# Attention stage without elementwise work on GpSimd, and low weight parts by an adding DMA

## The chip, the cores and the metric

The kernel runs on one core of a Trainium2 chip. The metric is the device time of one execution in microseconds, the median of several runs. The engines are TensorE (PE, with its weight loads shown as PEld), VectorE (DVE), ScalarE (ACT), GpSimd (POOL) and SyncE (SP), which here only issues DMAs.

## The reference

One block of a bidirectional encoder on 512 tokens of width 1024, with 16 learned meta tokens in front, in float32:

```python
u = rms_norm(h, pre_mix_gain)
qa, ka, va, qb, kb, vb, g = split(u @ w_in)         # rope on qa, ka, qb, kb
o_swa  = windowed_gqa_sink_attention(qa, ka, va, sink)   # 16 heads of 64, 4 kv heads, +-128 and meta keys
o_diff = differential_attention(qb, kb, vb, lam)    # 8 heads: (softmax(q1 k1) - lam softmax(q2 k2)) v,
                                                    # then RMS norm of each head
gates = sigmoid(g + b_gate)
merged = gates[:D] * (o_swa @ w_branch_swa) + gates[D:] * (o_diff @ w_branch_diff)
h = h + rms_norm(merged @ w_out)
f = (silu(gate) * up) @ w_ffn_out                   # gate, up = rms_norm(h) @ w_ffn_in, 2816 wide each
h = h + rms_norm(f)
```

## The kernel before, in words

Every float32 operand of a large product is split into a high part that TensorE multiplies at full speed (`float32r`) and a low part, the difference. A product is hi\*hi + hi\*lo + lo\*hi, summed in PSUM (`mm3`, L139-144). Activations lie with features on the partitions (`xh`, `xl`: 8 slices of 128 features by 528 tokens); a projection is 8 slices of 3 matmuls into one PSUM bank `pr` (`proj_g`, L146).

**Weights** come in tiles of 128 x 1024 floats (512 KB) by `load_w` (L124): SP loads `raw` (tile `wr`, 3 buffers), ACT casts it to the high part `wh` (L130), and the low part `wl` = raw - wh is a subtraction in `sub_hi` (L110). For the 4th to the 51st call POOL does three quarters of that subtraction (768 columns) and DVE the last quarter (256); for all others DVE does all 1024. `wh` and `wl` have 3 buffers each, so ACT can write the parts of a load when the product three loads back has ended.

**Windowed attention** (`s_swa`, L448, and `t_swa`, L502) runs over 16 units, each a query block of 128 tokens by 4 heads. Per head TensorE makes scores (L465), DVE adds the mask and takes the minimum (L468; scores are negated), and ACT takes the exponential with its sum (L471). The sink sits in one more column of the tile `p`, which POOL fills head by head (L467). Then DVE inverts the sums and POOL scales the four heads' probabilities (L476). TensorE transposes them (L516), ACT casts the high part `ah` (L115), DVE makes the low part `al` (L111), and TensorE multiplies them by V (L530-534).

**Differential attention** (`s_diff`, L607, and `t_diff`, L645) runs over 8 heads of 4 query blocks with two score maps each: scores `Sd` into one double bank (L626), minimum `dnm` on DVE (L629), exponential on ACT (L630). For a query block DVE makes the two factors `drc` (L634-635), POOL scales the first map (L636) and DVE adds the second (L638, tile `pa` or `pp`). After transposes and the products with V the head is normed over its rows: square on ACT, its low part `sl` on POOL (L683), a power by logarithm and exponential, and a Newton step with three operations on POOL (L699-701) and one on DVE (L702).

**Rotary embedding** (`rope`, L321): two products on DVE (`ta`, `tb`, L325-326), their sum on POOL (L327), then a split into `hl` on ACT and DVE (L118-119), from which SP's DMAs build the operands `Q`, `Qd`, `Kd`. It is called 26 times.

**Fillers.** Between the steps of attention TensorE takes projections: queries, keys and values of coming heads (`f_q`, `f_qk`, `f_vd`), the gates (`f_gate`, 8 beside windowed attention and 8 near the end of the differential branch in `f_gate2`), and the product with `w_branch_swa` (`f_b1`, 8 tiles, beside the first heads). The class `Order` (L35) fixes in which order TensorE takes all these pieces, from written costs and delays; that order does not depend on the other engines' code. On DVE, ACT, POOL and SP a scheduler orders the instructions after the first part of the kernel when the program is built, each queue then running in that order.

After about 550 us the branch products, the output projection and the FFN follow, with no such interleaving.

Of the kernel before, what the change touches and what calls it, by code (L numbers as in the profile page):

```python
# [12 lines left out]
F32 = mybir.dt.float32  # L13
# [7 lines left out]
P = 128  # L21
# [74 lines left out]
def encoder(ctx, tc, I, out, dbg=None):  # L96
# [25 lines left out]
    nw = [0]  # L122

    def load_w(src, k=KT, dst=None):  # L124
        raw = wp.tile([P, k, D // k], F32, tag="wr", name="wr", bufs=RB)
        sp.dma_start(out=raw, in_=src.rearrange("p (k c) -> p k c", k=k))
        if dst is None:
            dst = [wp.tile([P, k, D // k], F32R, tag=t, name=t) for t in ("wh", "wl")]
        wh, wl = dst
        act.copy(out=wh, in_=raw)  # L130
        # during attention the vector engine is the busiest: GpSimd takes three quarters of the low parts
        nw[0] += 1
        cut = 3 * k // 4 if 4 <= nw[0] < 52 else 0
        if cut:
            sub_hi(wl[:, 0:cut], raw[:, 0:cut], wh[:, 0:cut], pool)
        sub_hi(wl[:, cut:], raw[:, cut:], wh[:, cut:])
        return wh, wl
# [18 lines left out]
    def rsqrt_cols(pl, ss, n, scale, tag, extra=None, bufs=1):  # L156
        """(ss*scale + eps)^-0.5 on [n, m] columns, with one Newton step; extra replaces eps."""
        m = ss.shape[1]
        v, h, y, z = (pl.tile([P, m], F32, tag=tag + c, name=tag + c, bufs=bufs) for c in "vhyz")
        if extra is None:  # L160
            dve.tensor_scalar(out=v[:n], in0=ss, scalar1=scale, scalar2=EPS, op0=ALU.mult, op1=ALU.add)
        else:
            dve.scalar_tensor_tensor(out=v[:n], in0=ss, scalar=scale, in1=extra, op0=ALU.mult, op1=ALU.add)  # L163
        pool.tensor_tensor(out=y[:n], in0=v[:n], in1=mhalf[:n, 0:m], op=ALU.pow)  # L164
        dve.tensor_scalar(out=h[:n], in0=v[:n], scalar1=-0.5, scalar2=1.0, op0=ALU.mult, op1=ALU.mult)
        if m == 1:
            dve.scalar_tensor_tensor(out=z[:n], in0=y[:n], scalar=h[:n], in1=y[:n], op0=ALU.mult, op1=ALU.mult)
        else:
            dve.tensor_tensor(out=z[:n], in0=y[:n], in1=y[:n], op=ALU.mult)
            dve.tensor_tensor(out=z[:n], in0=z[:n], in1=h[:n], op=ALU.mult)  # L170
        dve.scalar_tensor_tensor(out=y[:n], in0=z[:n], scalar=1.5, in1=y[:n], op0=ALU.add, op1=ALU.mult)
        return y

# [14 lines left out]
    zero = const.tile([P, 256], F32, name="zero")  # L188
# [4 lines left out]
    RB = 3  # L193
# [18 lines left out]
    # the tensor engine's clock rises only under load  # L212
# [59 lines left out]
    # K of the windowed branch, slice by slice as x arrives; then V  # L272
# [13 lines left out]
    # row statistics of x: 1/rms, broadcast to all partitions  # L286
# [28 lines left out]
    # small vectors  # L315
# [5 lines left out]
    def rope(hl, psa, psb, c0, n, o0, scale=None):  # L321
        """psa, psb: [P, n] products of columns c0..c0+n; hl[:, part, hi/lo, o0..o0+n] gets the rotated split."""
# [4 lines left out]
        pool.tensor_tensor(out=ta, in0=ta, in1=tb, op=ALU.add)  # L327
# [53 lines left out]
    def v_swa(VT):  # L381
# [6 lines left out]
        act.copy(out=m, in_=zero[0:48, :].rearrange("p (a b c) -> p a b c", a=2, b=2))  # L388
# [43 lines left out]
    # per query block: (key column range, mask, [(offset in range, key block or -1 for meta)])  # L432
# [10 lines left out]
    # meta rows of the transposed probabilities; the gaps between the row groups stay zero  # L443
    aTm = atp.tile([80, 512], F32R, tag="am", name="aTm")
    for c in range(2):
        act.copy(out=aTm[:, c * 256:(c + 1) * 256], in_=zero[0:80, :])

    def s_swa():  # L448
        for u in range(16):
# [9 lines left out]
            pt = atp.tile([P, 4, 401], F32, tag="p", name="p", bufs=2)  # L459
            for hh in range(4):  # L460
# [6 lines left out]
                pool.tensor_copy(out=p[:, nk:nk + 1], in_=nsink[:, h:h + 1])  # L467
# [7 lines left out]
            for hh in range(4):  # L475
                pool.tensor_scalar(out=pt[:, hh, 0:nk], in0=pt[:, hh, 0:nk], scalar1=rc[:, hh:hh + 1],  # L476
                                   scalar2=1.0, op0=ALU.mult, op1=ALU.mult)
# [5 lines left out]
    def pipe(n, tr_fn, av_fn, done_tr, free_at):  # L483
        """tr_fn(k), then av_fn(k, operand): two transposed banks ahead."""
# [64 lines left out]
    def f_gate(j, dst):  # L549
        w = load_w(I["w_in"][36 + j])  # L550
# [33 lines left out]
    def f_vd(h):  # L584
# [8 lines left out]
        def finish():  # L593
# [5 lines left out]
            act.copy(out=m, in_=zero[0:80, 0:P])  # L599
# [7 lines left out]
    def s_diff():  # L607
        for h in range(8):
# [8 lines left out]
            for i in range(4):  # L617
# [4 lines left out]
                for c in range(2):  # L622
                    S = ps.tile([P, 2, 512], F32, tag="S", name="Sd")
                    for s in range(2):
                        for x in range(2):
# [10 lines left out]
                pool.tensor_scalar(out=pc[0], in0=pc[0], scalar1=rc[:, 0:1], scalar2=1.0,  # L636
                                   op0=ALU.mult, op1=ALU.mult)
# [7 lines left out]
    def t_diff():  # L645
        free_at = 0.0
        for h in range(8):
# [28 lines left out]
            # per-head RMS norm over the 128 rows of O  # L676
# [6 lines left out]
            split(sh, sl, sq, eng=pool)  # L683
# [15 lines left out]
            pool.tensor_tensor(out=z, in0=y, in1=y, op=ALU.mult)  # L699
            pool.tensor_tensor(out=z, in0=z, in1=v, op=ALU.mult)  # L700
            pool.tensor_scalar(out=z, in0=z, scalar1=-0.5, scalar2=1.5, op0=ALU.mult, op1=ALU.add)
            dve.tensor_tensor(out=y, in0=y, in1=z, op=ALU.mult)  # L702
# [21 lines left out]
    def f_b1(j):  # L724
        w = load_w(I["w_bs"][j])
# [68 lines left out]
    # the eight banks as two sets of four  # L794
# [25 lines left out]
    # all of w_out stays on chip, in the space of the hidden activations  # L820
# [236 lines left out]
```

## Time and profile before

| | |
|---|---|
| three runs | 1016.4, 1016.48, 1017.12 us (median 1016.48) |
| span of the profiled execution | 1015.2 us |
| busy TensorE | 973.6 us (96%) |
| busy DVE, ACT, POOL | 589.3, 446.8, 246.8 us |

The time listed is that of the runs; for the profiled execution only its span is given. "Busy" counts instructions at work; matmuls are pipelined and their ends modelled, so TensorE's busy time hides short waits. A row of a group shows line, engine, operation, tiles (out<-in), shapes and count, then busy time and mean ns, then idle time before and what ended it. A row of the timeline shows start and duration in us, and in brackets the engine's idle time before it with what it waited for.

### The profile page before, as it was taken

The numbers are of one execution on the slowest core, as the hardware profiler recorded it, in microseconds if no ns is written. First come the engines' busy times: TensorE is split into PE (matmuls) and PEld (weight loads), VectorE is DVE, ScalarE is ACT, GpSimd is POOL, SyncE is SP. The second block draws the span as 40 slices with busy tenths as digits, with TensorE's granted clock in tenths as the row PEclk, the third lists the DMA queues.
The fourth block names the chain that finished last, engine by engine and source line by source line (L and its number), as shares of the span: only waits on it lengthen the run. The fifth ranks groups of instructions, "written<-read, shape, count | busy, mean of one in ns | idle before, by whom it ended". The sixth has DMA issues, their size and how long they took to land.

```text
span 1015.2 us, 14301 instructions
## 1 busy us (share of the span) xinstructions
PE 973.6 (96%) x5355; PEld 830.5 (82%) x5355; DVE 589.3 (58%) x979; ACT 446.8 (44%) x820; POOL 246.8 (24%) x294
## 2 busy tenths in 40 slices
PE   9989999989999997998999999999999999999997
PEld 9767777869888887988887888998888888888885
DVE  5856788766675868788874574863333333322224
ACT  6336677565443654654556352543233233222121
POOL 1443454534434554543421000100000000000000
PEclk9998999999999999998999999999999999999999
DMA  9572131341515144233512471353323323324122
GB/s 329 157 196 71 43 83 43 92 117 46 146 61 147 43 126 123 57 100 100 145 59 90 134 230 56 112 175 104 102 86 104 102 84 104 102 86 145 57 68 83
DMA packets 36597, 109.33 MB, mean 108 GB/s; under 512 B 5921, under 2 KB 6433, under 8 KB 35889
## 3 DMA queue, kind: packets, MB, share of 16 engines
q1 hardware_dynamic: 36528, 108.42, 35.3%
q8 instruction: 42, 0.69, 0.3%
q14 instruction: 27, 0.21, 0.1%
HBM read 87.04 MB, written 2.10 MB: 88 GB/s over the span
## 4 chain that ended last, share of the span: by engine, by line
PE 73%; DVE 12%; DMA 4%; issue 4%; ACT 4%; POOL 2%; SPq 1%; DVEq 0%; ACTq 0%; POOLq 0%
PE pr L142 15%; PE pr L143 15%; PE pr L144 15%; PE wk L142 2%; PE wk L143 2%; PE wk L144 2%; PE tr L516 2%; DMA wr<-in_w_in_dram 2%; PE Sd L626 2%; DVE wl L111 2%; PE Sw L465 2%; PE acc L143 1%; PE tr L143 1%; PE acc L142 1%; PE tr L142 1%
## 5 line engine op out<-in xcount | busy, mean ns | idle before, releaser
L130 ACT CAST wh<-wr 128x1024 fp32r<-128x1024 f32 x134 | 140.7, 1051 | 279.1 <-PE pr L143 122.2
L111 DVE TENSOR_TENSOR wl<-wr,wh 128x1024 fp32r<-128x1024 f32 (+2 forms) x138 | 153.1, 1110 | 138.3 <-ACT wh L130 130.5
L142 PE MATMUL pr<-xh,wh 128*128 128x264 f32 (+1 forms) x616 | 199.9, 325 | 0.0
L143 PE MATMUL pr<-xl,wh 128*128 128x264 f32 (+1 forms) x616 | 197.7, 321 | 0.7 <-DVE xl L234 0.7
L144 PE MATMUL pr<-xh,wl 128*128 128x264 f32 (+1 forms) x616 | 197.4, 320 | 0.7 <-DVE wl L111 0.7
L144 PEld LDWEIGHTS pr<-xh,wl 128*128 128x128 f32 x616 | 117.0, 190 | 9.3 <-DVE wl L111 0.9
L143 PEld LDWEIGHTS pr<-xl,wh 128*128 128x128 f32 x616 | 117.2, 190 | 7.1 <-DVE xl L234 1.2
L142 PEld LDWEIGHTS pr<-xh,wh 128*128 128x128 f32 x616 | 117.1, 190 | 6.9 <-issue 1.2
L111 POOL TENSOR_TENSOR wl<-wr,wh 128x768 fp32r<-128x768 f32 x48 | 95.6, 1992 | 86.9 <-ACT wh L130 85.0
L142 PE MATMUL pr<-uh,wh 128*128 128x512 f32 (+1 forms) x304 | 110.8, 364 | 0.0
L143 PE MATMUL pr<-ul,wh 128*128 128x512 f32 (+1 forms) x304 | 110.6, 364 | 0.0
L144 PE MATMUL pr<-uh,wl 128*128 128x512 f32 (+1 forms) x304 | 110.6, 364 | 0.0
L164 POOL TENSOR_TENSOR r3y<-r3v,mhalf 128x1 f32<-128x1 f32 x4 | 2.2, 552 | 352.7 <-DVE r3v L163 352.7
L142 PEld LDWEIGHTS pr<-uh,wh 128*128 128x128 f32 x304 | 57.3, 189 | 9.1
L144 PEld LDWEIGHTS pr<-uh,wl 128*128 128x128 f32 x304 | 57.4, 189 | 9.1
L143 PEld LDWEIGHTS pr<-ul,wh 128*128 128x128 f32 x304 | 57.4, 189 | 9.0
L629 DVE TENSOR_REDUCE dnm<-Sd 128x1 f32<-128x528 f32 x64 | 44.9, 702 | 22.8 <-PE Sd L626 22.5
L626 PE MATMUL Sd<-Kd,Qd 128*128 128x264 f32 x256 | 44.4, 295 | 9.6 <-ACT pp L630 8.0
L471 ACT ACTIVATE p<-p,nm 128x273 f32<-128x273 f32 (+1 forms) x64 | 36.9, 576 | 30.9 <-DVE nm L468 21.9
L468 DVE CUSTOM_DVE_ANT_0 p<-Sw,mk,nsink 128x272 f32<-128x272 f32 (+1 forms) x64 | 36.0, 563 | 24.3 <-PE Sw L465 22.9
L327 POOL TENSOR_TENSOR ta<-ta,tb 128x528 f32<-128x528 f32 (+1 forms) x26 | 35.7, 1372 | 55.0 <-DVE tb L326 46.4
L626 PEld LDWEIGHTS Sd<-Kd,Qd 128*128 128x128 f32 x256 | 36.7, 191 | 14.4 <-ACT pp L630 11.4
(370 smaller groups left out, 1979.3 us busy)
## 6 DMA issues: line engine op xcount, KB each, us to landing
wr<-in_w_in_dram SPq DMA_DIRECT2D x50, 512.0 KB, 3.8
wr<-in_w_fi_dram SPq DMA_DIRECT2D x50, 512.0 KB, 3.5
wr<-in_w_fo_dram SPq DMA_DIRECT2D x22, 512.0 KB, 3.5
Kd<-hl SPq DMA_DIRECT2D x32, 132.0 KB, 2.4
Kd<-Kd SPq DMA_DIRECT2D x8, 528.0 KB, 4.3
Q<-hl SPq DMA_DIRECT2D x64, 64.0 KB, 2.0
Qd<-hl SPq DMA_DIRECT2D x64, 64.0 KB, 2.1
wr<-in_w_bs_dram SPq DMA_DIRECT2D x8, 512.0 KB, 3.5
```

The costliest lines, as they stand in the source:

```text
L111: (eng or dve).tensor_tensor(out=lo, in0=src, in1=hi.bitcast(F32), op=ALU.subtract)
L130: act.copy(out=wh, in_=raw)
L142: pe.matmul(out=ps, lhsT=ah, rhs=bh, start=first, stop=False)
L143: pe.matmul(out=ps, lhsT=ah, rhs=bl, start=False, stop=False)
L144: pe.matmul(out=ps, lhsT=al, rhs=bh, start=False, stop=last)
L327: pool.tensor_tensor(out=ta, in0=ta, in1=tb, op=ALU.add)
L465: pe.matmul(out=S, lhsT=Qs[g][hh // 2][:, hh % 2, i * P:(i + 1) * P], rhs=KK[g // 2][:, c, g % 2, r0:r1], start=(c == 0), stop=(c == 1))
L468: dve.tensor_tensor_reduce(out=p[:, 0:nk], in0=S, in1=mask, scale=1.0, scalar=nsink[:, h:h + 1], op0=ALU.add, op1=ALU.min, accum_out=nm[:, ...
L471: act.activation(out=p, in_=p, func=AF.Exp, scale=-1.0, bias=nm[:, hh:hh + 1], accum_out=den[:, hh:hh + 1])
L516: pe.transpose(out=tr[0:kk, hh * P:(hh + 1) * P], in_=pt[:, hh, o:o + kk], identity=ident)
L626: pe.matmul(out=S[:, s, 0:HALF], lhsT=Q[:, c, i * P:(i + 1) * P], rhs=K[:, x, c, s * HALF:(s + 1) * HALF], start=(x == 0), stop=(x == 1))
L629: dve.tensor_reduce(out=nm[:, c:c + 1], in_=S[:, :, 0:HALF], axis=AX.XY, op=ALU.min)
```

## The change

- `load_w` no longer splits the subtraction between POOL and DVE. By default DVE does all of it. With `by_dma` (the 16 gate loads in `f_gate` and the 8 loads of `w_branch_swa` in `f_b1`) ACT writes -raw, rounded, into `wl`, and a DMA that POOL issues adds `raw` to it in place.
- `raw` has 4 buffers in place of 3. To make room, the tile `zero` has 1 column in place of 256 and is read as a broadcast.
- The rotary sum, the scaling of the first differential map and the low part of the squares go from POOL to DVE; the scaling of windowed probabilities goes from POOL to ACT.
- The sink column is filled once for a unit's four heads, ahead of its scores, still on POOL.
- The Newton step becomes a square on ACT and two operations on DVE in place of three on POOL and one on DVE.

The costs and delays of `Order` stay, and TensorE's instructions stand in the same order as before.

```diff
-    def load_w(src, k=KT, dst=None):
+    def load_w(src, k=KT, dst=None, by_dma=False):
...
         act.copy(out=wh, in_=raw)
-        nw[0] += 1
-        cut = 3 * k // 4 if 4 <= nw[0] < 52 else 0
-        if cut:
-            sub_hi(wl[:, 0:cut], raw[:, 0:cut], wh[:, 0:cut], pool)
-        sub_hi(wl[:, cut:], raw[:, cut:], wh[:, cut:])
+        if by_dma:
+            act.activation(out=wl, in_=raw, func=AF.Copy, scale=-1.0)
+            pool.dma_start(out=wl.bitcast(F32), in_=raw, accum_op=ALU.add)
+        else:
+            sub_hi(wl, raw, wh)
...
-    zero = const.tile([P, 256], F32, name="zero")
+    zero = const.tile([P, 1], F32, name="zero")
...
-    RB = 3
+    RB = 4
...
-        pool.tensor_tensor(out=ta, in0=ta, in1=tb, op=ALU.add)
+        dve.tensor_tensor(out=ta, in0=ta, in1=tb, op=ALU.add)
...
             pt = atp.tile([P, 4, 401], F32, tag="p", name="p", bufs=2)
+            pool.tensor_copy(out=pt[:, :, nk], in_=nsink[:, 4 * g:4 * g + 4])
             for hh in range(4):
...
-                pool.tensor_copy(out=p[:, nk:nk + 1], in_=nsink[:, h:h + 1])
...
             for hh in range(4):
-                pool.tensor_scalar(out=pt[:, hh, 0:nk], in0=pt[:, hh, 0:nk], scalar1=rc[:, hh:hh + 1],
-                                   scalar2=1.0, op0=ALU.mult, op1=ALU.mult)
+                act.activation(out=pt[:, hh, 0:nk], in_=pt[:, hh, 0:nk], func=AF.Copy, scale=rc[:, hh:hh + 1])
...
-        w = load_w(I["w_in"][36 + j])
+        w = load_w(I["w_in"][36 + j], by_dma=True)
...
-                pool.tensor_scalar(out=pc[0], in0=pc[0], scalar1=rc[:, 0:1], scalar2=1.0,
-                                   op0=ALU.mult, op1=ALU.mult)
+                dve.tensor_scalar(out=pc[0], in0=pc[0], scalar1=rc[:, 0:1], scalar2=None, op0=ALU.mult)
...
-            split(sh, sl, sq, eng=pool)
+            split(sh, sl, sq)
...
-            pool.tensor_tensor(out=z, in0=y, in1=y, op=ALU.mult)
-            pool.tensor_tensor(out=z, in0=z, in1=v, op=ALU.mult)
-            pool.tensor_scalar(out=z, in0=z, scalar1=-0.5, scalar2=1.5, op0=ALU.mult, op1=ALU.add)
-            dve.tensor_tensor(out=y, in0=y, in1=z, op=ALU.mult)
+            act.activation(out=z, in_=y, func=AF.Square)
+            dve.scalar_tensor_tensor(out=z, in0=z, scalar=-0.5, in1=v, op0=ALU.mult, op1=ALU.mult)
+            dve.scalar_tensor_tensor(out=y, in0=z, scalar=1.5, in1=y, op0=ALU.add, op1=ALU.mult)
...
-        w = load_w(I["w_bs"][j])
+        w = load_w(I["w_bs"][j], by_dma=True)
```

Three places show how the queues change (lines of the changed kernel are 2 to 5 lower). The first is DVE in differential attention, sixth head, from the minimum of one score map to that of the next (`dnm` minimum, `hl` rotated queries and keys, `VT` scaled values, `pa` probabilities). Before:

```order
L629 TENSOR_REDUCE dnm<-Sd 128x1
L111 TENSOR_TENSOR wl<-wr,wh 128x256
L119 SCALAR_TENSOR_TENSOR hl<-ta,qsc,hl 128x2x264
L363 TENSOR_TENSOR VT<-pr,rbc 128x264
L638 SCALAR_TENSOR_TENSOR pa<-pp,drc,pa 128x528
L629 TENSOR_REDUCE dnm<-Sd 128x1
```

And in the changed kernel, at the same minimum (`z` is the Newton step):

```order
L626 TENSOR_REDUCE dnm<-Sd 128x1
L632 TENSOR_TENSOR drc<-drc,nlam 128x1
L633 TENSOR_SCALAR pa<-pa,drc 128x528
L111 TENSOR_TENSOR wl<-wr,wh 128x1024
L696 SCALAR_TENSOR_TENSOR z<-z,v 128x512
L634 SCALAR_TENSOR_TENSOR pa<-pp,drc,pa 128x528
L119 SCALAR_TENSOR_TENSOR hl<-ta,qsc,hl 128x2x264
L361 TENSOR_TENSOR VT<-pr,rbc 128x264
L626 TENSOR_REDUCE dnm<-Sd 128x1
```

The factor `drc` has moved behind the first minimum, the scaling and a Newton operation came from POOL, and the low part has 1024 columns in place of 256.

The second is ACT in windowed attention, sixth unit (`p` exponentials, `otmp` and `oh` output, `aTm` and `ah` high parts of transposed probabilities). Before:

```order
L471 ACTIVATE p,den<-p,nm 128x401
L544 COPY otmp<-O 64x256
L471 ACTIVATE p,den<-p,nm 128x401
L115 CAST oh<-of 128x2x128
L115 CAST aTm<-tr 16x512
L115 CAST ah<-tr 128x512
L471 ACTIVATE p,den<-p,nm 128x401
L115 CAST ah<-tr 128x512
```

And now:

```order
L469 ACTIVATE p,den<-p,nm 128x401
L541 COPY otmp<-O 64x256
L469 ACTIVATE p,den<-p,nm 128x401
L115 CAST oh<-of 128x2x128
L115 CAST aTm<-tr 16x512
L115 CAST ah<-tr 128x512
L469 ACTIVATE p,den<-p,nm 128x401
L474 ACTIVATE p<-p,rc 128x400 x4
L115 CAST ah<-tr 128x512
```

The four scalings stand between the last exponential of a unit and the next cast that TensorE's products need.

The third is POOL. Now, from the first sink columns of windowed attention to its last adding DMA, it holds only this:

```order
L458 COPY p<-nsink 128x4 x2
L162 TENSOR_TENSOR r0y<-r0v,mhalf 128x5
L132 DMA wl<-wr 128x1024 x4
L458 COPY p<-nsink 128x4 x3
L132 DMA wl<-wr 128x1024
L458 COPY p<-nsink 128x4
L132 DMA wl<-wr 128x1024
L458 COPY p<-nsink 128x4 x8
L132 DMA wl<-wr 128x1024 x2
L458 COPY p<-nsink 128x4 x2
L132 DMA wl<-wr 128x1024 x16
```

Where low parts, rotary sums and scalings stood between the sink columns, adding DMAs stand, each of which waits in the queue for ACT's copy.

More of the change, by code (lines that the diff above doesn't have):

```diff
@@ L120, in split @@
                                      op0=ALU.mult, op1=ALU.subtract)
-    nw = [0]
-    def load_w(src, k=KT, dst=None):
+    def load_w(src, k=KT, dst=None, by_dma=False):
         raw = wp.tile([P, k, D // k], F32, tag="wr", name="wr", bufs=RB)
@@ L387, in v_swa @@
         m = atp.tile([48, 2, 2, 64], F32R, tag="vm", name="Vm", bufs=2)
-        act.copy(out=m, in_=zero[0:48, :].rearrange("p (a b c) -> p a b c", a=2, b=2))
+        act.copy(out=m, in_=zero[0:48].unsqueeze(2).unsqueeze(3).broadcast_to([48, 2, 2, 64]))
         msrc = tm[0:NMETA, 0:P].rearrange("p (g e) -> p g e", g=2)
@@ L445, in encoder @@
     for c in range(2):
-        act.copy(out=aTm[:, c * 256:(c + 1) * 256], in_=zero[0:80, :])
+        act.copy(out=aTm[:, c * 256:(c + 1) * 256], in_=zero[0:80].broadcast_to([80, 256]))
     def s_swa():
@@ L598, in finish @@
             m = atp.tile([80, P], F32R, tag="vm", name="Vdm", bufs=2)
-            act.copy(out=m, in_=zero[0:80, 0:P])
+            act.copy(out=m, in_=zero[0:80].broadcast_to([80, P]))
             split(m[0:16], m[32:48], tm[0:NMETA, 0:P])
```

## The prediction

> **What bounds the kernel now.** I read the page first, then the busy time by stage, then who waits for whom on TensorE's weight loads, then the timeline at one of the longest waits. The page's line of the engines:
>
> ```profile
> span 1015.2 us, 14301 instructions
> PE 973.6 (96%) x5355; PEld 830.5 (82%) x5355; DVE 589.3 (58%) x979; ACT 446.8 (44%) x820; POOL 246.8 (24%) x294
> ```
>
> TensorE (PE) bounds the kernel: the change can win only time in which PE waits or runs slowly, and lose by making it wait more. Where that is, the table by stretch says (columns: us, then busy us of PE, its weight loads, DVE, ACT, POOL; granted clock; DMA):
>
> ```profile
> 60.00:245.00 185.00, 170.84 (x944) 138.19 (x943) 133.01 (x300) 114.86 (x269) 84.62 (x144) 0.98 0.28 80
> 245.00:500.00 255.00, 238.24 (x1622) 216.24 (x1620) 192.04 (x299) 129.94 (x253) 122.34 (x92) 0.99 0.36 99
> 550.00:600.00 50.00, 50.00 (x221) 41.28 (x221) 31.57 (x38) 25.82 (x33) 2.97 (x3) 1.00 0.45 141
> 89.00:97.00 8.00, 7.17 (x23) 5.87 (x24) 4.17 (x12) 2.51 (x6) 2.87 (x8) 0.57 0.20 66
> 461.00:469.00 8.00, 6.60 (x34) 6.31 (x33) 7.48 (x13) 2.72 (x7) 3.37 (x4) 0.57 0.79 200
> ```
>
> 60 to 245 is windowed attention, 245 to 500 differential attention. PE idles 185 - 170.84 = 14.2 us in the first and 255 - 238.24 = 16.8 us in the second, and none once attention is over (50.00 of 50.00). Twice 8 us run at a granted clock of 0.57, so 8 x 0.43 = 3.4 us are lost each time. All that can be won is 14.2 + 16.8 + 6.9 = 38 us, and a little that the modelled ends of matmuls hide. What the weight loads wait for between 60 and 550 (us in total, times, longest):
>
> ```profile
> PEld Sd L626 <- ACT pp L630: 11.4, 10, 1.8
> PEld O L534 <- DVE aTm L111: 7.5, 7, 2.5
> PEld O L531 <- DVE al L111: 4.9, 8, 1.5
> PEld Od L143 <- DVE dal L111: 4.3, 7, 1.1
> PEld tr L658 <- DVE Vd L111: 4.1, 2, 2.2
> PEld Sw L465 <- DMA Q<-hl: 3.1, 1, 3.1
> ```
>
> The largest is scores of the differential branch that wait for ACT's exponential to free their bank. Before one such wait DVE, then POOL, then ACT did this; the last two rows of DVE show two of the same instructions elsewhere:
>
> ```profile
> 453.78 0.69 DVE L629 TENSOR_REDUCE dnm<-Sd 128x1 f32<-128x528 f32 x1
> 454.39 0.72 DVE L111 TENSOR_TENSOR wl<-wr,wh 128x256 fp32r<-128x256 f32 x1
> 455.04 1.21 DVE L119 SCALAR_TENSOR_TENSOR hl<-ta,qsc,hl 128x528 fp32r<-128x528 f32 x1
> 456.17 0.42 DVE L363 TENSOR_TENSOR VT<-pr,rbc 128x264 f32<-128x264 f32 x1
> 456.51 2.00 DVE L638 SCALAR_TENSOR_TENSOR pa<-pp,drc,pa 128x528 f32<-128x528 f32 x1
> 458.44 0.69 DVE L629 TENSOR_REDUCE dnm<-Sd 128x1 f32<-128x528 f32 x1
> ...
> 461.57 0.41 DVE L111 TENSOR_TENSOR wl<-wr,wh 128x256 fp32r<-128x256 f32 x1
> ...
> 382.44 0.77 DVE L638 SCALAR_TENSOR_TENSOR pa<-pp,drc,pa 128x528 f32<-128x528 f32 x1
> ...
> 381.75 0.15 DVE L635 TENSOR_TENSOR drc<-drc,nlam 128x1 f32<-128x1 f32 x1
> ```
>
> ```profile
> 455.66 2.29 POOL L111 TENSOR_TENSOR wl<-wr,wh 128x768 fp32r<-128x768 f32 x1
> ...
> 459.23 0.70 ACT L630 ACTIVATE pp<-Sd,dnm 128x528 f32<-128x528 f32 x1 [3.93 <-DVE dnm L629]
> ```
>
> DVE's `pa` takes 2.00 us here and 0.77 elsewhere: it ends just after POOL's low part does (455.66 + 2.29 = 457.95), so an instruction of DVE with two inputs in SBUF stands still while POOL reads there. The minimum `dnm` behind it is late, and ACT with it by 3.93 us. That is what the change goes at.
>
> **Part by part.** The groups by form, 60 to 550 us, carry the prices:
>
> ```profile
> L111 DVE TENSOR_TENSOR wl<-wr,wh 128x256 fp32r<-128x256 f32 x43 | 37.7, 876 | 6.5 <-ACT wh L130 6.2 <-DMA Q<-hl 0.3
> L638 DVE SCALAR_TENSOR_TENSOR pa<-pp,drc,pa 128x528 f32<-128x528 f32 x24 | 29.0, 1206 | 5.0 <-POOL pa L636 4.6
> L635 DVE TENSOR_TENSOR drc<-drc,nlam 128x1 f32<-128x1 f32 x32 | 17.1, 535 | 0.9
> L111 DVE TENSOR_TENSOR wl<-wr,wh 128x1024 fp32r<-128x1024 f32 x8 | 10.4, 1298 | 1.6 <-ACT wh L130 1.5
> L326 DVE TENSOR_TENSOR tb<-pr,rot 128x528 f32<-128x528 f32 x16 | 11.2, 703 | 3.2 <-PE pr L144 3.0
> L111 POOL TENSOR_TENSOR wl<-wr,wh 128x768 fp32r<-128x768 f32 x43 | 85.8, 1995 | 79.8 <-ACT wh L130 77.9 <-PE Sd L626 1.9
> L130 ACT CAST wh<-wr 128x1024 fp32r<-128x1024 f32 x51 | 53.4, 1048 | 44.9 <-PE pr L143 24.5 <-issue 7.6 <-DMA wr<-in_w_in_dram 7.2
> L471 ACT ACTIVATE p<-p,nm 128x401 f32<-128x401 f32 x32 | 20.2, 630 | 12.5 <-DVE nm L468 8.9 <-POOL p L467 3.3
> L471 ACT ACTIVATE p<-p,nm 128x273 f32<-128x273 f32 x32 | 16.7, 523 | 18.3 <-DVE nm L468 13.1 <-POOL p L467 4.0 <-POOL p L476 1.3
> L476 POOL TENSOR_SCALAR p<-p,rc 128x400 f32<-128x400 f32 x32 | 19.2, 619 | 16.0 <-DVE rc L474 16.0
> L476 POOL TENSOR_SCALAR p<-p,rc 128x272 f32<-128x272 f32 x32 | 15.9, 518 | 9.6 <-DVE rc L474 9.6
> ```
>
> *DVE loses its standstills.* Mean less the undisturbed row: 43 x (0.876 - 0.41) = 20.0, 24 x (1.206 - 0.77) = 10.5, 32 x (0.535 - 0.15) = 12.3; together 43 us.
>
> *DVE gains work.* Of the 48 loads whose low part POOL shared, 31 come wholly to DVE: 31 x (1.30 - 0.41) = 27.6. The other 17 (8 gates, 8 of `w_bs`, one late gate) leave it for the adding DMA (17 x 0.41 = 7.0), and so do the last 7 gates, which were whole on DVE (7 x 1.30 = 9.1). That nets +11.5. The 26 rotary sums at 0.70 (the product `tb` of the same size) are +18.2. The 32 scalings of differential probabilities are not in the trace on DVE: between 0.15 (the smallest row) and 0.70 (`tb`, which reads one operand more), so 5 to 22; I take 0.5, nearer the row of the same size, so 16. Low part of the squares and one more step of the norm, 8 x 0.7 each: +11. In all +57, against 43 that go: DVE gets 14 us more (bounds 3 and 20), on 133 + 192 = 325. The Trainium skill ("VectorE: DVE Perf Modes", Mode 2x_2P) says that a float32 operation with one tensor source in SBUF runs at two elements per cycle: by its 0.96 GHz I estimate 0.28 us for 528 elements, which would make the scalings 9 us rather than 16; no row of this trace shows that mode.
>
> *So the gain is not less work but smaller single delays*, and it is uneven. In the place above (rows of the order stand with the change) DVE had 0.69 + 0.72 + 1.21 + 0.42 + 2.00 = 5.0 us by its rows from one `dnm` to the next, 4.66 by starts (458.44 - 453.78). Now it has `dnm` 0.69, `drc` 0.15, scaling 0.5, a whole low part 1.30, a norm step 0.7, `pa` 0.77, `hl` 0.77 and `VT` 0.42: 5.3, and by starts (0.08 less each, as 0.69 became 454.39 - 453.78 = 0.61) 4.7. No gain there: the low part that stood beside DVE on POOL now stands on it. Where no whole low part falls between two `dnm`, up to 2 us go. Of the waits behind this queue (11.4 + 4.3 + 4.1 = 19.8) I take a third: **-7** (bounds +2 and -20).
>
> *ACT gains work.* 64 scalings of windowed probabilities at the exponential's price of the same shape, 32 x 0.63 + 32 x 0.523 = 36.9; 24 negated copies at 1.048 = 25.2; 8 squares at about 0.63 = 5. In windowed attention that is 36.9 + 8 x 1.048 = 45.3, and ACT goes from 114.9 to 160 of 185 us: 87% (about 83% by starts). It also sends the casts `ah`, `aTm`, `oh` that PE waits for through DVE (7.5 + 4.9), and four scalings in a row are 2.1 to 2.5 us during which those casts stand behind. Against that POOL's four (2.1 to 2.5 as well) were beside ACT. DVE's standstills go here too. Bounds: -5 (a third of 14.2 goes) and +13 (each of 16 units late by a third of 2.4 us); I take **+3**.
>
> *First queries.* The wait for `Q<-hl`, 3.1 us, hangs on two rotary sums. They fall from POOL's price to 0.70, and no low part of 1.995 stands ahead on POOL: **-1.5**.
>
> *The adding DMA.* No such transfer is in the trace. Nearest are a load of the same 512 KB and a copy of 528 KB inside SBUF:
>
> ```profile
> wr<-in_w_in_dram SPq DMA_DIRECT2D x50, 512.0 KB, 3.8
> Kd<-Kd SPq DMA_DIRECT2D x8, 528.0 KB, 4.3
> ```
>
> Since it reads both operands I bound it by 3.8 and 2 x 4.3 = 8.6 and take 6. A low part is then ready 1.05 + 1.05 + 6 = 8 us after its buffers come free, where it was 1.05 + 2. Cover in `f_b1`: the casts `wh` follow each other by
>
> ```profile
> 267.89 1.05 ACT L130 CAST wh<-wr 128x1024 fp32r<-128x1024 f32 x1 [1.80 <-PE pr L143]
> ...
> 274.37 1.05 ACT L130 CAST wh<-wr 128x1024 fp32r<-128x1024 f32 x1 [1.80 <-issue]
> ```
>
> 6.5 us, and with three buffers a cast has two products, 13 us, until its own product starts. So **0**; without that cover, 8.6 and a busy ACT, 24 times up to 0.5. Behind a waiting DMA on POOL stand only the sink columns, needed by the exponentials of two units later. The raw tile is held 5 us longer, and a fourth buffer answers that: SP's queue (rows for `Qd`, `Kd` stand behind such loads) isn't held. The Trainium skill ("SBUF — State Buffer", the "DVE blocks DMA" trap) speaks against the change: GpSimd cannot write a DMA's descriptors while DVE runs an operation of the two-port mode, and the new scalings would be such. By that rule a DMA is late by one scaling at most, which the cover swallows; no row shows it.
>
> Sum: -7 + 3 - 1.5 + 0 = -5.5 us. The span was 1015.2, so 1009.7; the median of the runs, 1016.48, lies 1.3 above it, so 1011, and I say **1010.5**.
>
> **Rivals.**
> *ACT takes POOL's place as the late engine (slower).* One mechanism: in windowed attention ACT stands above about 85% busy, each block of four scalings delays the casts, and PE waits for `al` and `aTm`. For it: 160 of 185. Against: DVE was at 133 there with 14 us of PE waits, and by starts ACT stays near 83%. It decides if casts come later than the 2 us that a block lasts. Price +13, with half the gain behind it (-3.5 - 1.5): 1016.5 + 8 = **1024**.
> *The standstills are the whole story.* Every wait behind DVE in differential attention goes (-19.8), the first queries too (-1.5), and with 458 to 462 the second stretch at 0.57 (-3.4): 1016.5 - 24.7 = **992**. For it: each of the longest waits has a DVE row over 2 us next to POOL's low part. Against: DVE's sum doesn't fall.
> *The adding DMA is late.* At 8.6 us, behind two copies in a busy ACT queue, the 24 loads come late by 0.4 on the mean (0.5 is the bound above, a little less where other work lies between): 1010.5 + 24 x 0.4 = **1020**.
> *Nothing moves.* DVE's queue is as long as it was, and what POOL did beside it is now in it: **1016**.
>
> **How the numbers follow.** A run of this kernel can tell about 0.2%, 2 us, from no change. Chances: the forecast 0.34, ACT late 0.26, the whole story 0.20, late DMA 0.08, nothing 0.12. Faster: 0.32 of the forecast, 0.20, 0.02 of nothing, so 0.54. Within 0.2%: 0.02 and 0.09, so 0.11. The rest, 0.35, slower. The range reaches to 990 (a little under the second rival) and 1025 (a little over the first); the forecast's own is 1003 to 1015.
>
> **What would show it.** Right: DVE's `pa`, `drc` and `hl` at 0.77, 0.15 and 0.77 throughout; DVE's busy time in attention about unchanged; ACT near 155 in the windowed stage; waits of `Sd` on ACT down by a third, those of `O` not; PE idle 245 to 500 near 10. Wrong: weight loads waiting for `wl` of a DMA; PE idle in the windowed stage far from 17; the stretch at 0.57 near 461 gone.

## The result, and the profile after

The changed kernel takes 1046.43 us (median of 4 runs, 1045.88 to 1046.99) where the kernel before took 1016.8 beside it: a ratio of 1.0288, 95% interval 1.0273 to 1.0302. The forecast was 1010.5; it was wrong in sign, and the time lies outside the range. The page of the changed kernel:

```profile
span 1044.1 us, 14069 instructions
PE 982.5 (94%) x5355; PEld 834.9 (80%) x5355; DVE 575.3 (55%) x1029; ACT 501.3 (48%) x916; POOL 37.1 (4%) x68
```

The table by stretch, with columns as before:

```profile
60.00:245.00 185.00, 161.55 (x852) 128.71 (x851) 119.54 (x285) 139.10 (x323) 8.28 (x19) 0.94 0.38 97
245.00:500.00 255.00, 235.74 (x1603) 213.15 (x1603) 184.89 (x333) 139.28 (x264) 7.78 (x8) 0.99 0.43 111
500.00:550.00 50.00, 42.57 (x230) 35.34 (x228) 27.42 (x52) 30.37 (x53) 4.63 (x5) 0.93 0.57 136
```

PE now idles 23.5 us in the first row (14.2 before) and 7.4 in the third (0.3 before), and the granted clock fell. Over the whole program:

```profile
core 0: 1015.2 us, clock 0.991
```

```profile
core 0: 1044.1 us, clock 0.981
```

The first is before, the second after. If all time at a lower clock counts as lost, that was 1015.2 x 0.009 = 9.1 us and is now 1044.1 x 0.019 = 19.8: by this estimate 10.7 of the 28.9 us lost come by the clock and 18 by waits. What the weight loads wait for between 60 and 550 us (total, times, longest):

```profile
PEld Sd L623 <- ACT pp L627: 12.8, 12, 2.2
PEld O L531 <- DVE aTm L111: 11.4, 10, 1.9
PEld Sw L464 <- DMA Q<-hl: 7.9, 1, 7.9
...
PEld Sd L623 <- DMA Kd<-Kd: 3.3, 1, 3.3
```

The wait for the first queries has grown from 3.1 to 7.9 us, and there is a new one for keys of the differential branch. No row names the `wl` of the adding DMA: the products never waited for it.

The standstills of DVE are gone. The place that the prediction shows (from one `dnm` to the next), in the timeline of the changed kernel:

```profile
469.10 0.71 DVE L626 TENSOR_REDUCE dnm<-Sd 128x1 f32<-128x528 f32 x1
469.72 0.15 DVE L632 TENSOR_TENSOR drc<-drc,nlam 128x1 f32<-128x1 f32 x1
469.79 0.49 DVE L633 TENSOR_SCALAR pa<-pa,drc 128x528 f32<-128x528 f32 x1
470.20 1.22 DVE L111 TENSOR_TENSOR wl<-wr,wh 128x1024 fp32r<-128x1024 f32 x1
471.33 0.68 DVE L696 SCALAR_TENSOR_TENSOR z<-z,v 128x512 f32<-128x512 f32 x1
471.94 0.76 DVE L634 SCALAR_TENSOR_TENSOR pa<-pp,drc,pa 128x528 f32<-128x528 f32 x1
472.61 0.76 DVE L119 SCALAR_TENSOR_TENSOR hl<-ta,qsc,hl 128x528 fp32r<-128x528 f32 x1
...
473.64 0.70 DVE L626 TENSOR_REDUCE dnm<-Sd 128x1 f32<-128x528 f32 x1
```

From minimum to minimum that is 473.64 - 469.10 = 4.54 us, forecast 4.7, before 4.66. DVE as a whole is busy for 575.3 us, 14 less than before.

And the DMAs (size, median us to landing), after and then before:

```profile
wl<-wr POOLq DMA_DIRECT2D x24, 512.0 KB, 5.6
Kd<-hl SPq DMA_DIRECT2D x32, 132.0 KB, 4.5
...
Qd<-hl SPq DMA_DIRECT2D x64, 64.0 KB, 3.7
```

```profile
Kd<-hl SPq DMA_DIRECT2D x32, 132.0 KB, 2.4
...
Qd<-hl SPq DMA_DIRECT2D x64, 64.0 KB, 2.1
```

The adding DMA lands in 5.6 us, but the small transfers from which differential scores are made take nearly twice as long.

TensorE's order is the same in all these kernels, so each matmul has its counterpart, and the start of the one less the start of the other tells where time is lost. This table, worked out from the traces, gives for a time in the kernel before how late (us) each kernel is there; e1 to e12 are the experiments below:

```
before   after     e1     e8    e11     e3     e4    e12
    57    -0.9   -1.0   -1.4   -1.1   -1.0   -1.0   -1.5
    80     5.3   -1.8    4.1    4.0    5.8   -1.9   -2.2
   100     3.2   -3.8    2.0    1.9    1.9   -5.8   -6.1
   245    13.3    2.4    8.3    9.1    0.6   -7.0   -5.9
   280    14.8    2.4   10.4   15.3    2.1   -7.0   -5.9
   345    19.0    0.6   10.5   19.0    6.3   -8.8   -8.0
   495    17.9   -1.3    8.0   17.0    5.1  -10.8  -12.8
   510    24.7   -0.3   14.3   23.6   11.6  -10.3  -13.9
   570    28.6    3.1   16.0   27.0   15.6   -8.6  -11.9
```

The loss has four places: +6 at the first queries (57 to 80), +10 in windowed attention (100 to 245), +6 beside the first differential heads (245 to 345), +11 around the late gates (495 to 570). Between 345 and 495, where no adding DMA runs, the change wins 1. One caution for all that follows: apart from TensorE, each kernel's queues are ordered anew when it is built, so an edit can also move instructions that it doesn't name.

### The profile page after: what moved, and what is told of

The parts are those of the page before. It is cut to its first block, busy times and chain, and to the rows that moved or that the text cites. A ratio compares the mean times of both kernels' runs of the same rounds, so it can differ in the third digit from the quotient of the medians.

```text
span 1044.1 us, 14069 instructions
## 1 busy us (share of the span) xinstructions
PE 982.5 (94%) x5355; PEld 834.9 (80%) x5355; DVE 575.3 (55%) x1029; ACT 501.3 (48%) x916; POOL 37.1 (4%) x68
## 4 chain that ended last, share of the span: by engine, by line
PE 71%; DVE 11%; ACT 7%; DMA 5%; issue 3%; SPq 2%; DVEq 0%; ACTq 0%; POOLq 0%
PE pr L140 15%; PE pr L141 15%; PE pr L142 15%; PE wk L141 2%; PE wk L142 2%; PE wk L140 2%; PE Sd L623 2%; DMA Kd<-hl 2%; PE tr L141 1%; PE tr L140 1%; PE tr L142 1%; PE tr L513 1%; PE Sw L464 1%; DVE wl L111 1%; PE acc L141 1%
## 5 line engine op out<-in xcount | busy, mean ns | idle before, releaser
L111 DVE TENSOR_TENSOR wl<-wr,wh 128x1024 fp32r<-128x1024 f32 (+1 forms) x114 | 137.0, 1203 | 135.0 <-ACT wh L128 126.3
L623 PEld LDWEIGHTS Sd<-Kd,Qd 128*128 128x128 f32 x256 | 37.0, 194 | 25.2 <-ACT pp L627 14.2
L464 PE MATMUL Sw<-KK,Q 128*128 128x272 f32 (+1 forms) x128 | 33.3, 342 | 7.6 <-DMA Q<-hl 7.5
L627 ACT ACTIVATE pp<-Sd,dnm 128x528 f32<-128x528 f32 x40 | 27.8, 695 | 23.6 <-DVE dnm L626 23.2
L132 POOL DMA_DIRECT2D wl<-wr x24 | 22.7, 947 | 375.8 <-ACT wl L131 306.2
```

Of the source, the lines that this page charges most:

```text
L111: (eng or dve).tensor_tensor(out=lo, in0=src, in1=hi.bitcast(F32), op=ALU.subtract)
L132: pool.dma_start(out=wl.bitcast(F32), in_=raw, accum_op=ALU.add)
L464: pe.matmul(out=S, lhsT=Qs[g][hh // 2][:, hh % 2, i * P:(i + 1) * P], rhs=KK[g // 2][:, c, g % 2, r0:r1], start=(c == 0), stop=(c == 1))
L623: pe.matmul(out=S[:, s, 0:HALF], lhsT=Q[:, c, i * P:(i + 1) * P], rhs=K[:, x, c, s * HALF:(s + 1) * HALF], start=(x == 0), stop=(x == 1))
L627: act.activation(out=p.rearrange("p (a b) -> p a b", a=2), in_=S[:, :, 0:HALF], func=AF.Exp, scale=-1.0, bias=nm[:, c:c + 1], accum_out=de ...
```

## The experiments

Theory A: the adding DMA is the main cause. Theory B: ScalarE's longer queue. Theory C: VectorE's longer queue. Ratios are to the kernel before, run beside each; 0.001 is 1 us.

### e1: low parts of the 24 loads on VectorE

```diff
-        w = load_w(I["w_in"][36 + j], by_dma=True)
+        w = load_w(I["w_in"][36 + j])
...
-        w = load_w(I["w_bs"][j], by_dma=True)
+        w = load_w(I["w_bs"][j])
```

> The changed kernel with the low parts of the 24 loads on VectorE, as for every other weight: no adding DMA, no negated copy on ScalarE (24 x 1.05 = 25 us less there), 24 x 1.30 = 31 us more on VectorE; the rest of the change stays. Theory A, the adding DMA is the main cause (a raw buffer held until it lands, with SyncE's queue behind it, and the late gates beside its traffic): the +5 at 60 us and the +11 at 500 to 550 go, about 1030. Theory B, ScalarE's longer queue is the main cause and the scalings of windowed attention its larger part: only a few us go, about 1040. Theory C, VectorE's queue decides: 31 us more on it, slower than the changed kernel, about 1052.

1020.47 us, ratio 1.0031 (1.0017 to 1.0045): 26 us of the 29 are gone, more than any theory gave. A holds; C falls, since VectorE has more work than in the changed kernel (601.3 us against 575.3) and the time is shorter.

### e2: the adding DMA alone, in the kernel before

```diff
+        if by_dma:
+            act.activation(out=wl, in_=raw, func=AF.Copy, scale=-1.0)
+            pool.dma_start(out=wl.bitcast(F32), in_=raw, accum_op=ALU.add)
+            return wh, wl
```

with `by_dma` for the same 24 loads and the changed kernel's `zero` and `RB = 4`.

> The kernel before with one part of the change: the 24 loads of gate and windowed branch output weights get their low part by negated copy and adding DMA, with the fourth raw buffer (and the smaller zero tile that makes room for it); all else stays on GpSimd as before. Theory A: most of the loss comes with it, about 1038. Theory B: only the 24 copies of ScalarE's added work are in, about 1022. Theory C: VectorE and GpSimd are relieved of 24 low parts, faster than before, about 1008.

1034.44 us, 1.0167 (1.0151 to 1.0183). By itself, with its copies and the fourth buffer, it costs 17 us in a kernel that it relieves of work on VectorE and GpSimd, nearer A's 1038 than any other. Why it is 17 here and 26 beside the rest of the change was not tried apart.

### e3: windowed scalings back on GpSimd; e4: that and e1

```diff
-                act.activation(out=pt[:, hh, 0:nk], in_=pt[:, hh, 0:nk], func=AF.Copy, scale=rc[:, hh:hh + 1])
+                pool.tensor_scalar(out=pt[:, hh, 0:nk], in0=pt[:, hh, 0:nk], scalar1=rc[:, hh:hh + 1],
+                                   scalar2=1.0, op0=ALU.mult, op1=ALU.mult)
```

> The changed kernel with the 64 scalings of windowed probabilities back on GpSimd (37 us less on ScalarE between 60 and 245 us), the rest of the change stays. Theory A: the windowed stage's +8 shrinks a little, about 1042. Theory B: the +8 goes, and some of what its delay carries on, about 1034. Theory C: VectorE stands still again beside GpSimd's scalings in few places, 1046.

> The changed kernel with both undone: low parts of the 24 loads on VectorE, windowed scalings on GpSimd. What stays of the change is the rotary sums, the differential scalings, the whole low parts, the low part of the squares and the norm step on VectorE or ScalarE. Theory A and B together: 1012 to 1020, about the kernel before. Theory C: about 1050, since VectorE's work is the same as with the low parts alone on it.

e3: 1032.55 us, 1.0144 (1.0124 to 1.0163). e4: 1009.48 us, 0.9923 (0.9903 to 0.9943). The scalings on ScalarE cost 1.0288 - 1.0144 = 14 us with the adding DMA and 1.0031 - 0.9923 = 11 without it, nearly all between 100 and 245 us (the table). So B holds as the second cause; e4 came out a little below what A and B together gave. Windowed attention in e1, then in e4:

```profile
60.00:245.00 185.00, 167.99 (x919) 135.43 (x919) 131.92 (x302) 141.24 (x330) 3.68 (x14) 0.97 0.28 80
```

```profile
60.00:245.00 185.00, 174.30 (x996) 142.15 (x996) 139.48 (x314) 118.83 (x272) 38.59 (x78) 1.00 0.28 82
```

ACT at 141 of 185 us (76%) costs PE 6 us of idle and some clock; at 119 it doesn't. And e4 is faster than the kernel before: what is left of the change is a gain.

### e5: ScalarE's copies without the DMA

```diff
-            pool.dma_start(out=wl.bitcast(F32), in_=raw, accum_op=ALU.add)
+            dve.tensor_tensor(out=wl, in0=wl.bitcast(F32), in1=raw, op=ALU.add)
```

> The changed kernel with ScalarE's 24 negated copies kept, but VectorE instead of the DMA adds the raw weights to them (24 x 1.30 us on VectorE as in e1, which took 1020.5). Apart from e1 only the 24 copies of 1.05 us on ScalarE, and the wait of each sum for its copy, are in. Theory A1, the copies are what the adding DMA's 26 us consist of: about 1040. Theory A2, the transfers' traffic is, and theory A3, the raw buffers held until a transfer lands are: about 1022 to 1025.

1026.32 us, 1.0105 (1.0078 to 1.0132): 7 us over e1 by the ratios, 6 by the medians. So the copies are the smaller part of the 26: A1, that they are all of it, falls.

### e6: only the last 8 gates without the adding DMA

```diff
-        w = load_w(I["w_in"][36 + j], by_dma=True)
+        w = load_w(I["w_in"][36 + j], by_dma=j < NB)
```

> The changed kernel with the last 8 gates' low parts on VectorE; the first 8 gates and the 8 weights of the windowed branch's output keep the adding DMA. Every theory of the adding DMA has these late gates beside the last heads' Kd and Qd transfers: the delay that rises by 8.5 us at 503 to 510 us should stay at 1 to 2, so 1037 to 1039. If it stays at 1046, that rise comes from elsewhere (VectorE's or ScalarE's queue at that place).

1037.62 us, 1.0206 (1.0191 to 1.0222), as expected: 8 us belong to the late gates. How, DVE's and then ACT's timeline of the changed kernel show:

```profile
528.08 0.69 DVE L550 TENSOR_TENSOR z<-pr,rbc 128x512 f32<-128x512 f32 x1 [9.27 <-DMA Qd<-hl]
528.69 0.68 DVE L111 TENSOR_TENSOR dal<-tr,dah 128x512 fp32r<-128x512 f32 x1
529.28 0.70 DVE L626 TENSOR_REDUCE dnm<-Sd 128x1 f32<-128x528 f32 x1
```

```profile
530.01 0.70 ACT L627 ACTIVATE pa<-Sd,dnm 128x528 f32<-128x528 f32 x1 [8.44 <-DVE dnm L626]
```

The gate's result `z` is put where `hl` was, so it waits until the last head's `Qd` transfers have read `hl`. In DVE's queue `dal` and `dnm` stand behind it, and PE and ACT wait for those.

### e8: the traffic alone, beside e1

```diff
+            sub_hi(wl, raw, wh)
+            pool.dma_start(out=idle, in_=wl.bitcast(F32), accum_op=ALU.add)
...
-    RB = 4
+    RB = 3
+    idle = const.tile([P, KT, P], F32, name="idle")
+    pool.memset(idle, 0.0)
```

(for the 24 loads; `idle` is read by nobody.)

> The kernel of e1 (low parts on VectorE, 1020.5) and beside it 24 adding DMAs of 512 KB issued by GpSimd as in the changed kernel, from the finished low part into a tile that nobody reads, so that no product and no raw buffer waits for them (the tile takes the room of the fourth raw buffer). Theory A2, the traffic on the DMA engines slows SyncE's transfers of Q, Kd and Qd: 1035 to 1045. Theories A1 and A3: about 1021.

1034.1 us, 1.017 (1.0153 to 1.0188): 14 us more than e1, for transfers whose data no instruction needs. A2 holds, just below the expected 1035. The DMAs of e8:

```profile
idle<-wl POOLq DMA_DIRECT2D x24, 512.0 KB, 6.1
Kd<-hl SPq DMA_DIRECT2D x32, 132.0 KB, 3.5
...
Qd<-hl SPq DMA_DIRECT2D x64, 64.0 KB, 3.3
```

And DVE's same `z` as above, in e8 and then in e1:

```profile
516.81 0.69 DVE L552 TENSOR_TENSOR z<-pr,rbc 128x512 f32<-128x512 f32 x1 [6.36 <-DMA Qd<-hl]
```

```profile
503.16 0.69 DVE L550 TENSOR_TENSOR z<-pr,rbc 128x512 f32<-128x512 f32 x1 [2.04 <-DMA Qd<-hl]
```

By the table e8 loses against e1 at three of the four places: 6 us at the first queries, 4 beside the first differential heads (245 to 345) and 5 at the late gates (495 to 510). The wait for the first queries is 8.1 us in e8 (longest of its kind, 2.2 in e1):

```profile
PEld Sw L466 <- DMA Q<-hl: 8.1, 1, 8.1
```

### e14: is it the traffic, or the raw buffer less?

```diff
-    RB = 4
+    RB = 3
```

in e1.

> The kernel of e1 (low parts on VectorE, 1020.5) with three raw buffers instead of four. e8's 13.6 us over e1 are put down to the traffic of its transfers, but e8 has also one raw buffer less. If the buffer count does nothing where no transfer holds one: 1019 to 1022, and the 13.6 are traffic. If the fourth buffer is what counts: up to 1034.

1019.77 us, 1.0029 (1.0017 to 1.004), as e1. The buffer count does nothing there; e8's 14 us are traffic.

### e11: the same traffic, now holding the raw buffer

```diff
-            pool.dma_start(out=idle, in_=wl.bitcast(F32), accum_op=ALU.add)
+            pool.tensor_copy(out=idle[:, 0, 0:1], in_=wl[:, 0, 0:1].bitcast(F32))
+            pool.dma_start(out=idle, in_=raw, accum_op=ALU.add)
```

in e8.

> The kernel of e8 (1034.1) with its 24 transfers reading the raw weights instead of the low part, after a one-column copy on GpSimd that makes each follow its low part: same traffic, but now the raw buffer is held until the transfer lands, and there are three raw buffers. Theory A3, the raw buffer held with SyncE's queue behind it is what is left of the adding DMA's 26 us after the traffic (14) and the copies (6): 1040. Theory A2 alone: 1034.

1044.65 us, 1.0277 (1.0255 to 1.03): 11 us more than e8, most of it from 245 to 345 us in the table, and more than A3's 1040. One place shows how holding the buffer costs, in ACT's timeline of e11 and then in that of TensorE's weight loads:

```profile
278.67 1.04 ACT L128 CAST wh<-wr 128x1024 fp32r<-128x1024 f32 x1 [7.11 <-DMA wr<-in_w_bs_dram]
279.62 0.69 ACT L630 ACTIVATE pa<-Sd,dnm 128x528 f32<-128x528 f32 x1
```

```profile
280.45 0.94 PEld L626 LDWEIGHTS Sd<-Kd,Qd 128*128 128x128 f32 x4 [4.90 <-ACT pa L630]
```

The load of this cast went out at 256.41 us in e8, ahead of a head's `Qd` transfers. In e11 an adding DMA holds its buffer until 262.70, SP's queue has the load behind those transfers, and it goes out at 272.03. Its cast waits 7.11 us for it, the exponential stands behind the cast in ACT's queue, and TensorE waits 4.90 us for the exponential (2.33 there in e8). So part of the price is order: at two heads one load fewer stands ahead of the `Qd` transfers (31 and 39 in place of e8's 32 and 40).

The changed kernel has four raw buffers, its SP queue has as many loads ahead of those transfers as e1 (33 and 41), and none of ACT's waits between 60 and 570 us names a load. SP does wait for adding DMAs there. Its largest wait from 40 to 620 us, in the changed kernel and then before:

```profile
SPq L124 <- DMA wl<-wr: 174.0, 15, 24.5
```

```profile
SPq L126 <- DVE wl L111: 287.0, 34, 18.4
```

So a wait of SP is no loss by itself: before the change SP waited for raw buffers about as long (by all its rows some 330 us, now some 350). A wait costs only where transfers behind the load were ready. One such place in the changed kernel, in SP's timeline and then in ACT's:

```profile
309.39 19.74 SPq L124 DMA_DIRECT2D wr<-in_w_in_dram  x2
329.23 1.84 SPq L576 DMA_DIRECT2D Qd<-hl  x2
```

```profile
327.29 0.74 ACT L118 ACTIVATE hl<-ta,qsc 128x528 fp32r<-128x528 f32 x1 [0.26 <-DVE ta L325]
```

SP spends 19.74 us on the issue of two loads, since the second waits for a raw buffer that an adding DMA still reads. But `hl` was made only at 327.29 + 0.74 = 328.03, so `Qd` went out 1.2 us late, not 19.74. Before the change every such `Q` or `Qd` behind a load went out 0.02 to 0.03 us after its `hl`; in the changed kernel four of eleven were late, by 0.9 to 1.9 us, 5 us together. PE's 3.3 us wait for `Kd<-Kd` follows here, and the hold is the smaller part of it: `Kd<-Kd` was issued 9.9 us after `hl`, where e1 has 6.3.

Of the 26 us that e1 showed, copies (7) and traffic (14) leave about 5 for the hold in the changed kernel. e11's 11 us are a price with three buffers and another order; how much of the 5 is the hold was not tried apart.

### e9 and e10: what sharing low parts with GpSimd costs

e9 is e4 with three quarters of 48 low parts on POOL, as before; e10 is the kernel before with all of them whole on DVE. The edits of e9, then of e10:

```diff
-            sub_hi(wl, raw, wh)
+            nw[0] += 1
+            cut = 3 * k // 4 if 4 <= nw[0] < 52 else 0
+            if cut:
+                sub_hi(wl[:, 0:cut], raw[:, 0:cut], wh[:, 0:cut], pool)
+            sub_hi(wl[:, cut:], raw[:, cut:], wh[:, cut:])
```

```diff
-        cut = 3 * k // 4 if 4 <= nw[0] < 52 else 0
+        cut = 0
```

> The kernel of e4 (1009.5) with three quarters of the low parts of 48 weights back on GpSimd, as in the kernel before; rotary sums, differential scalings, low part of the squares and the norm step stay on VectorE and ScalarE. Tells what the sharing with GpSimd was worth. If VectorE's standstills beside GpSimd's low parts cost what the prediction's differential term says: 1013 to 1017, about the kernel before. If VectorE standing still is free there because less work is on it: 1008 to 1010.

> The kernel before with one thing changed: no low part is shared with GpSimd, all are whole on VectorE (48 x 0.89 = 43 us more undisturbed work there). GpSimd keeps rotary sums, scalings, the low part of the squares and the norm step. Theory S, the sharing is what costs, since a quarter on VectorE beside GpSimd's three quarters takes as long as the whole: most of what e4 won, 1005 to 1012. Theory R, the other moves (rotary sums, differential scalings) won it, and VectorE gets longer by the whole low parts: 1016 or slower.

e9: 1035.25 us, 1.0185 (1.0162 to 1.0207), 26 us slower than e4, far more than expected. e10: 1009.33 us, 0.9934 (0.9912 to 0.9956), as theory S has it: the sharing costs. The low parts in e9, then in e4:

```profile
L111 DVE TENSOR_TENSOR wl<-wr,wh 128x256 fp32r<-128x256 f32 x43 | 54.2, 1261 | 3.1 <-ACT wh L130 3.0
```

```profile
L111 DVE TENSOR_TENSOR wl<-wr,wh 128x1024 fp32r<-128x1024 f32 x52 | 63.5, 1221 | 10.1 <-ACT wh L128 9.8
```

A quarter on DVE beside POOL's three takes 1.26 us, the whole on DVE alone 1.22: the sharing saved nothing. In the kernel before that quarter took 0.876 on the mean; seven of its 43 quarters ran apart from POOL's part there, three in e9, which explains only some of the difference. So in e9 the sharing costs more than in the kernel before; that this is why e9 lost so much is argued from these rows, not tried apart.

### e12: differential scalings on GpSimd; e15: the norm too

```diff
-                dve.tensor_scalar(out=pc[0], in0=pc[0], scalar1=rc[:, 0:1], scalar2=None, op0=ALU.mult)
+                pool.tensor_scalar(out=pc[0], in0=pc[0], scalar1=rc[:, 0:1], scalar2=1.0,
+                                   op0=ALU.mult, op1=ALU.mult)
```

in e4. e15 also takes the low part of the squares and the Newton step back to POOL, as they stand in the kernel before:

```diff
-            split(sh, sl, sq)
+            split(sh, sl, sq, eng=pool)
...
-            act.activation(out=z, in_=y, func=AF.Square)
-            dve.scalar_tensor_tensor(out=z, in0=z, scalar=-0.5, in1=v, op0=ALU.mult, op1=ALU.mult)
-            dve.scalar_tensor_tensor(out=y, in0=z, scalar=1.5, in1=y, op0=ALU.add, op1=ALU.mult)
+            pool.tensor_tensor(out=z, in0=y, in1=y, op=ALU.mult)
+            pool.tensor_tensor(out=z, in0=z, in1=v, op=ALU.mult)
+            pool.tensor_scalar(out=z, in0=z, scalar1=-0.5, scalar2=1.5, op0=ALU.mult, op1=ALU.add)
+            dve.tensor_tensor(out=y, in0=y, in1=z, op=ALU.mult)
```

> The kernel of e4 (1009.5) with the 32 scalings of differential probabilities back on GpSimd (VectorE loses 32 x 0.49 = 16 us, and its pa has to wait for GpSimd's 0.78). If VectorE's queue is what PE's differential waits hang on: 1002 to 1007. If the hand-over there and back costs more than the work: 1010 to 1014.

> The kernel of e12 (1004.1) with the low part of the squares and the three norm steps back on GpSimd, as in the kernel before (VectorE loses 8 x 0.7 + 8 x 0.7 = 11 us, ScalarE 8 squares). If the prediction's term for them (+11 us on VectorE, little of it on the path) is right: 1002 to 1005. If GpSimd's longer chain for the norm is late for the heads behind it: 1005 to 1009.

e12: 1004.06 us, 0.9878 (0.9862 to 0.9894), the fastest of all: the scalings on VectorE cost e4 about 4.5 us. e15: 1007.1 us, 0.9894 (0.9877 to 0.991), in the range expected for a norm that is late on GpSimd; by the medians moving it wins 3 us, but the intervals overlap.

### e13: windowed scalings on VectorE

```diff
-                pool.tensor_scalar(out=pt[:, hh, 0:nk], in0=pt[:, hh, 0:nk], scalar1=rc[:, hh:hh + 1],
-                                   scalar2=1.0, op0=ALU.mult, op1=ALU.mult)
+                dve.tensor_scalar(out=pt[:, hh, 0:nk], in0=pt[:, hh, 0:nk], scalar1=rc[:, hh:hh + 1], scalar2=None,
+                                  op0=ALU.mult)
```

in e4.

> The kernel of e4 (1009.5) with the 64 scalings of windowed probabilities on VectorE instead of GpSimd (about 64 x 0.4 = 26 us, by the 0.49 of the differential scaling and 272 to 400 of its 528 columns), beside 140 of 185 us that VectorE works in that stage. ScalarE's 64 scalings cost 11 us (e1 against e4) with 24 us more on it than GpSimd's took. If the place of the scalings doesn't matter as long as the engine isn't ScalarE: 1008 to 1011. If any in-order engine that PE waits for pays: 1015 to 1022.

1019.44 us, 1.0024 (1.0015 to 1.0034): 10 us over e4, as much as on ScalarE, though the scalings take only 0.36 to 0.43 us here. What PE waits for from 60 to 245 us in e13, then in e4:

```profile
PEld Sw L464 <- DVE nm L466: 11.6, 20, 1.8
PEld O L532 <- DVE aTm L111: 9.0, 10, 1.6
```

```profile
PEld O L532 <- DVE aTm L111: 4.9, 4, 1.7
PEld Sw L464 <- DVE nm L466: 4.0, 11, 0.8
```

The same stage of e13 by engine:

```profile
60.00:245.00 185.00, 167.19 (x919) 132.38 (x919) 151.00 (x366) 114.60 (x266) 4.48 (x14) 1.00 0.28 79
```

ScalarE is at 115 us here, VectorE at 151. So ScalarE's load is not the point; the rows fit a block of scalings that delays what stands behind it, on either engine whose results PE waits for. That the delay comes from the block, and not from the queue's greater length, was not tried apart.

## Why the prediction was wrong

In steps, by ratio: before 1, whole low parts 0.9934 (e10), rotary sums, sink columns and buffers on top of that 0.9894 (e15), norm 0.9878 (e12), differential scalings 0.9923 (e4), windowed scalings 1.0031 (e1), adding DMA 1.0288. That is -7, -4, -2, +4.5, +11, +26 us. The intervals of the second step's two kernels barely miss each other and those of the third overlap. Another order of the steps would share the time out otherwise: the adding DMA is +26 as the last step and +17 alone (e2).

- **The adding DMA, taken at 0, measured +26.** This step failed. Its landing was sized right (5.6 us against 6), and its cover held: no product waits for its `wl`. But the prediction looked for the cost only at that product. It fell on others: by the traffic on `Q`, `Kd`, `Qd` (14 us, e8), by the copies (7, e5), and by about 5 that are left for the raw buffer. "The fourth buffer answers that, SP's queue isn't held" failed too, at a small price: four `Qd` transfers went out 0.9 to 1.9 us late. The waits that the prediction named first as its own refutation (weight loads on `wl`) did not come, so that sign was badly chosen; another, PE idle far from 17 us in the windowed stage, did (23.5).
- **Windowed attention, taken at +3 with a bound of +13, measured +11 to +14.** The step was mis-sized, and the first rival had the size, in part by luck. Its condition was wrong: ACT stood at 76% (e1), not above 85%, although the scalings took what they were priced at (0.62 and 0.51 us against 0.63 and 0.52), and e13 shows the same price with DVE as the engine. The prediction set against it that POOL's scalings took as long; but in e4, with the scalings on POOL, none of PE's waits in this stage names POOL.
- **Differential attention, taken at -7.** All the standstills went: `pa` 0.76, `drc` 0.15, `hl` 0.76 us. In the changed kernel only 1 us was won from 345 to 495 us, in e4 2, and without the differential scalings on VectorE 5 (e12). From 245 to 495, e4 won 4. Whole low parts brought 7 us in e10 over the whole kernel. So the direction was right, the size for this term too large, and the scalings on VectorE took part of it back.
- **DVE's work, taken at +14 in attention, measured -14 over the whole program.** The prediction left out other two-input rows that stood still, `hl` (1.107 to 0.762 us, 16 times) and `pp` (1.085 to 0.760, 8 times) among them, 8 us in these two. Less work on VectorE did not make the kernel faster.
- **First queries, taken at -1.5, measured +6.** Without the adding DMA (e1, e4) they gain about 1 us; its traffic turns that round (e8, +5.5).
- **Late gates, not in the prediction: 8 us.** `z` waiting for `Qd` to leave its buffer was there in e1 with 2.04 us; with slower transfers it is 6.36 in e8 and 9.27 in the changed kernel.
- **The clock.** The prediction counted two stretches of 8 us at 0.57 as time that could be won. The changed kernel has more waits and more such time, 10.7 us of the loss by the mean; e12, the fastest, was granted 0.995. That the waits bring the lower clock is argued from this, not tried apart.

## What to carry to other kernels

A transfer moved off the engines is not free when nobody waits for its data: price the transfers that run beside it, the buffer that it keeps, and what stands in the issuing queue behind the load that wants that buffer. A busy share well below full (76% and 82% here) is no proof that a queue which PE waits for can take more work; ask first whether the old place of that work was slowing anything. A long wait in an issuing queue is not a cost either: compare it with the kernel before, and look when what stands behind it was ready. And sharing an elementwise operation between VectorE and GpSimd is worth a look at the mean of the small part: where it is as long as the whole one alone, the sharing can go.

## What the runs showed of the hardware

- An accumulating DMA of 512 KB inside SBUF landed in 5.1 (e11), 5.6 (the changed kernel) and 6.1 us (e8), by the medians. With 24 of them the median of the 64 KB transfers `Qd` went from 2.2 (e1) to 3.3 (e8) and that of the 132 KB `Kd` from 2.5 to 3.5, or to 3.7 and 4.5 in the changed kernel. In the runs without an adding DMA both lie between 2.0 and 2.8.
- VectorE's scaling of float32 by a column took 0.355 us for 272 elements, 0.425 for 400 (e13) and 0.487 for 528. That is (0.487 - 0.355) / 256 = 0.52 ns for an element and some 0.21 us for the instruction:

```profile
L474 DVE TENSOR_SCALAR p<-p,rc 128x400 f32<-128x400 f32 x32 | 11.5, 425 | 0.2
L474 DVE TENSOR_SCALAR p<-p,rc 128x272 f32<-128x272 f32 x32 | 9.4, 355 | 0.1
```

```profile
L633 DVE TENSOR_SCALAR pa<-pa,drc 128x528 f32<-128x528 f32 x24 | 11.7, 487 | 0.0
```

  The Trainium skill ("VectorE: DVE Perf Modes", Mode 2x_2P) has two elements per cycle, from which the prediction estimated 0.28 us for 528. The slope agrees with it, 0.52 ns at the prediction's 0.96 GHz; the estimate left out the fixed part.
- What the Trainium skill says on GpSimd's descriptors and the two-port mode ("SBUF — State Buffer", the "DVE blocks DMA" trap) no run here shows by itself. In e2 the differential scalings stay on GpSimd, and the adding DMA landed in 6.0 us there against 5.6 in the changed kernel, so the new scalings did not make it slower to land.
